# The recurrent stage's small matrix products: grouped by shape, head halves interleaved, fewer decay columns

## The chip, the cores and the metric

The kernel runs on one core of one Trainium2 chip, as one program. The metric is the device time of one execution in microseconds (us). The five engines work side by side: TensorE (PE: matrix products, its weight loads shown as PEld), VectorE (DVE), ScalarE (ACT), GpSimd (POOL) and SyncE (SP, which here issues the weight transfers).

## The reference, cut to what matters

Two transformer-like blocks work one after the other on 256 tokens of width 2048, all in float32. The first block has four kinds of attention and a gated feed-forward layer. The second has three branches; the change touches only the middle one, a recurrent time mix with 16 heads of width 64:

```python
w = -jax.nn.softplus(-(f(w0) + jnp.tanh(wd) @ f(w2))) - 0.5
decay = jnp.exp(-jnp.exp(w))
...
def step(state, inp):                      # one token, per head
    r_t, w_t, k_t, v_t, a_t, b_t = inp
    sa = jnp.einsum('bhij,bhj->bhi', state, a_t)
    state = state * w_t[:, :, None, :] + sa[..., None] * b_t[:, :, None, :] + v_t[..., None] * k_t[:, :, None, :]
    return state, jnp.einsum('bhij,bhj->bhi', state, r_t)
```

The kernel computes this in chunks of 64 tokens: within a chunk the products of all pairs of tokens are made at once (a "Gram" matrix per head and chunk), a triangular system is solved, and the 64x64 state is carried from chunk to chunk.

## The kernel before, in words

**The dense stream.** All wide projections (`unit_b`, `unit_a`) read their weights from HBM in pieces of 128x1024 float32 (512 KB, issued by SP at L291). ACT rounds a piece to a float32r copy `Wh` (L293), DVE makes the remainder `Wl` (L294). For each piece TensorE does 8 products with `Wh` (512 columns: activations in two parts) and 8 with `Wl` (256 columns), into the PSUM tiles `pd`. This stream runs from the first to the last microsecond, and every other piece of work is a small task that advances by one `yield` after each dense piece (`step`). All tiles `ps` are the side tasks' own four PSUM buffers. Every product is issued by the helper `mm` (L189) and every transpose by the helper `tr` (L193), so the trace shows these two lines and the tiles tell the work apart.

**The recurrent stage.** The 16 heads are 8 pairs: pair i has its two heads (h = 0, 1) on partitions 0-63 and 64-127. Four pairs are a group, so there are two groups; 256 tokens are 4 chunks.

- `rw_pre(i)`, for each of 8 pairs: the decays. `sig` (tokens by features) is multiplied by a constant triangle; `tri2` holds two of them side by side, one that includes the token itself and one that excludes it, so one product gives 256 columns. ACT takes the exponentials (L1215, both halves in one instruction, and L1217). Then come the Gram products (L1262): 4 chunks for head 0 on rows 0-63, then 4 for head 1 on rows 64-127; DVE masks each head's PSUM tile (L1265) and POOL writes a part of it to DRAM.
- `rw_solve`, `rw_merge`: the triangular solve, not touched.
- `rw_scan(g, c)`, for each group and chunk, 8 heads each: the values are brought to time-major order (below "V"; L1357 a product with the identity for head 0, L1358 a transpose for head 1, in turn); products `pw`, `pu`, `pn` with `yield`s between them; last the output `po` (L1407 and L1408): for every head the state's share (64 rows) and then the chunk's own share (128 rows), in turn, the second accumulating on the first. In chunk 0 there is no state's share.

In the trace a float32 product is two MATMUL records and a transpose is one; so 8 products of 64x64 are "x16". In the rows, `ps<-e,s` with 128*64 is `pn`, `ps<-s,q` with 64*64 is the state's share of `po`, `ps<-s,e` with 128*64 is the chunk's own share, `ps<-con,s` with 64*64 is V, `ps<-s,b` is the Gram product and `ps<-con,b` the four transposes after it.

**What sets the order.** The tile framework lists instructions per engine from the order of the code, by its own estimate of readiness; an instruction given to `pin` keeps its place. Each engine then works its list strictly in order.

Of the kernel before, what the change touches and what calls it, by code (L numbers as in the profile page):

```python
# [13 lines left out]
AF = mybir.ActivationFunctionType  # L14
OP = mybir.AluOpType
# [10 lines left out]
EM05 = float(np.exp(-0.5))  # L26
# [7 lines left out]
def shape_constants():  # L34

    p = np.arange(128)[:, None]
    c = np.arange(256)[None, :]
    dist = (128 + p - c).astype(np.float32)
    causal = dist >= 0

    def table(slope, ok):
        return np.where(ok, -np.float32(slope) * dist, np.float32(NEG)).astype(np.float32)

    def slopes(n):
        return (2.0 ** (-8.0 * np.arange(1, n + 1) / n)).astype(np.float32)

    tabs = [table(0.0, causal)]
    tabs += [table(s, causal) for s in slopes(8)]
    for h, s in enumerate(slopes(9)):
        win, dil = ((128, 1), (512, 4), (2048, 16))[h // 3]  # L50
        tabs.append(table(s, causal & (dist % dil == 0) & (dist <= win)))
    tabs += [table(s, causal) for s in slopes(4)]
    tabs = np.stack(tabs)

    i = np.arange(128)
    s64, c64 = i % 64, i // 64
    cons = {}
    cons["ident"] = np.eye(128)
    cons["ones"] = np.ones((128, 128))
    cons["bones"] = (c64[:, None] == c64[None, :])  # L60
    cons["anti"] = np.eye(128)[::-1]
    same = c64[:, None] == c64[None, :]
    incl = same & (s64[:, None] <= s64[None, :])
    excl = same & (s64[:, None] < s64[None, :])
    cons["tri2"] = -EM05 * np.concatenate([incl, excl], 1)
    cons["trif"] = (i[:, None] <= i[None, :])
    t64 = np.arange(64)
    cons["gmask"] = np.concatenate([s64[:, None] < t64[None, :], s64[:, None] <= t64[None, :]], 1)
    lm = []
    for b in (16, 32):  # L70
        lm.append((s64[:, None] // (2 * b) == t64[None, :] // (2 * b))
                  & (s64[:, None] // b % 2 == 0) & (t64[None, :] // b % 2 == 1))
    cons["lmask"] = np.concatenate(lm, 1)
    cons["qeye"] = np.tile(np.eye(16).reshape(1, 256), (128, 1))
    sel = np.zeros((128, 7, 128))
    for h in range(7):
        sel[h, h] = 1.0
    cons["sel7"] = sel.reshape(128, 896)
    cons["vmask"] = (i[:, None] // 16 == np.arange(8)[None, :])
    ctab = np.full((128, 2, 8, 16), NEG)  # L80
    cm = np.zeros((128, 2, 16))
    for qt in range(2):
        tq = qt * 128 + np.arange(128)
        dc = (tq[:, None] - (np.arange(15) * 16 + 31)[None, :]).astype(np.float32)
        for h, s in enumerate(slopes(8)):
            ctab[:, qt, h, :15] = np.where(dc >= 0, -s * dc, NEG)
        cm[:, qt, :15] = dc >= 0
    cons["ctab"] = ctab.reshape(128, 256)
    cons["cmask"] = cm.reshape(128, 32)
    out, off = [], {}  # L90
    for phase in PHASES:
        cols, parts = 0, []
        for k in phase:
            v = np.asarray(cons[k], np.float32)
            off[k] = (cols, v.shape[1])
            cols += v.shape[1]
            parts.append(v)
        out.append(np.ascontiguousarray(np.concatenate(parts, 1), np.float32))
    return tabs, out, off
# [2 lines left out]
PHASES = (("ident", "ones", "bones", "anti"),  # L102
          ("trif", "vmask", "ctab", "cmask"),
          ("sel7",),
          ("tri2", "gmask", "lmask"),
          ("qeye",))
TABS, CONST, COFF = shape_constants()

# [39 lines left out]
class Build:  # L148
# [1048 lines left out]
    def rw_pre(self, i, raw):  # L1197

        nc, v = self.nc, self.nc.vector
        V = self.V  # L1200
        st = self.rw[i] = {"vb": self.slot()}
        r, k, vv = (self.rw_lerp(raw[j], i, j) for j in range(3))
        del raw
        yield

        p = self.ps()
        p3 = p.rearrange("p (x t) -> p x t", x=2)
        for tt in range(2):
            self.mm(p3[:, :, tt * 128:tt * 128 + 128],
                    self.sig[tt][i // 4][:, (i % 4) * 128:(i % 4) * 128 + 128],  # L1210
                    self.C["tri2"].rearrange("p (x t) -> p x t", x=2))
        two = self.tmp((128, 1024), tag="b2")
        dec = two[:, :512]
        Pt, Pe = dec[:, :256], dec[:, 256:]
        nc.scalar.activation(dec, p, AF.Exp)  # L1215
        Pi = self.tmp()
        nc.scalar.activation(Pi, p[:, :256], AF.Exp, scale=-1.0)  # L1217
        st["pc"] = self.tiny(4)
        v.tensor_copy(st["pc"], Pt[:, 63:256:64])

        p = self.ps()[:, :256]
        self.mm(p, self.a2[i // 4][64:128, (i % 4) * 128:(i % 4) * 128 + 128], self.lad[64:128, :])
        a = self.tmp()
        nc.scalar.activation(a, p, AF.Tanh, scale=0.5, bias=V["a0"][:, i:i + 1])
        v.tensor_scalar(a, a, 0.5, 0.5, op0=OP.mult, op1=OP.add)

        q = self.tmp()
        nc.scalar.activation(q, k, AF.Square, scale=V["kk"][:, i:i + 1])
        yield
        p = self.ps()[:, :256]  # L1230
        self.mm(p, self.C["bones"], q)
        x = self.tmp()
        v.tensor_scalar(x, p, 1e-24, None, op0=OP.max)
        kn = self.tmp()
        self.rsqrt(kn, x, q)
        v.scalar_tensor_tensor(kn, k, V["kk"][:, i:i + 1], kn, op0=OP.mult, op1=OP.mult)
        ar = st["ar"] = self.slot((128, 4, 2, 64))
        bk = two[:, 512:].rearrange("p (c x t) -> p c x t", c=4, x=2)
        c4 = lambda t: t.rearrange("p (c t) -> p c t", c=4)
        v.scalar_tensor_tensor(ar[:, :, 0, :], c4(kn), -1.0, c4(Pe), op0=OP.mult, op1=OP.mult)  # L1240
        v.tensor_tensor(ar[:, :, 1, :], c4(r), c4(Pt), op=OP.mult)
        v.tensor_tensor(kn, kn, a, op=OP.mult)
        v.tensor_scalar(a, a, V["ka"][:, i:i + 1], self.ka1[:, i:i + 1], op0=OP.mult, op1=OP.add)
        v.tensor_tensor(k, k, a, op=OP.mult)
        for h in range(2):
            s = slice(64 * h, 64 * h + 64)
            v.tensor_tensor(bk[s, :, h, :], c4(kn[s]), c4(Pi[s]), op=OP.mult)
            v.tensor_tensor(bk[s, :, 1 - h, :], c4(k[s]), c4(Pi[s]), op=OP.mult)

        v.scalar_tensor_tensor(q, r, V["rk"][:, i:i + 1], k, op0=OP.mult, op1=OP.mult)  # L1250
        yield
        p = self.ps()[:, :256]
        self.mm(p, self.C["bones"], q)
        st["bv"] = st["vb"][:, 256:]
        v.tensor_tensor(st["bv"], p, vv, op=OP.mult)
        st["v"] = vv

        gm = st["gm"] = [self.slot((128, 4, 128)) for _ in range(2)]
        for h in range(2):
            s = slice(64 * h, 64 * h + 64)  # L1260
            p = self.ps()
            for c in range(4):  # L1262
                self.mm(p[:, c * 128:c * 128 + 128], bk[s, c].rearrange("p x t -> p (x t)"),
                        ar[s, c].rearrange("p x t -> p (x t)"))
            v.tensor_tensor(gm[h], p.rearrange("p (c t) -> p c t", c=4),  # L1265
                            self.C["gmask"][:, None, :].to_broadcast([128, 4, 128]), op=OP.mult)
            nc.gpsimd.dma_start(self.rd[i // 4, h, i % 4].rearrange("c s t -> s c t"), gm[h][s, :, 0:64])
        yield
        p = self.ps()
        for c in range(4):  # L1270
            self.tr(p[:, c * 128:c * 128 + 128], bk[:, c].rearrange("p x t -> p (x t)"))
        st["bkt"] = self.slot((128, 4, 128))
        nc.scalar.copy(st["bkt"], p.rearrange("p (c t) -> p c t", c=4))
# [68 lines left out]
    def rw_scan(self, g, c):  # L1342

        nc, v = self.nc, self.nc.vector
        R = [self.rw[4 * g + j] for j in range(4)]
# [8 lines left out]
        uv = [half(), half()]  # L1354
        p = self.ps().rearrange("p (j h t) -> p j h t", j=4, h=2)
        for j in range(4):
            self.mm(p[64:128, j, 0, :], R[j]["vb"][0:64, cs], self.ident[0:64, 0:64])  # L1357
            self.tr(p[0:64, j, 1, :], R[j]["vb"][64:128, cs], 64)  # L1358
        nc.scalar.copy(uv[0][64:128], p[64:128, :, 0, :])
        nc.scalar.copy(uv[1][0:64], p[0:64, :, 1, :])  # L1360
        yield
# [24 lines left out]
        if c < 3:  # L1386
# [13 lines left out]
            else:  # L1400
                v.tensor_tensor(sn, pn, bc, op=OP.mult)
            self.rwst = sn
        po = quad()
        for j in range(4):
            for h in range(2):
                s = hs[h]
                if c:  # L1407
                    self.mm(po[s, j, :], ST[s, j, :], R[j]["ar"][s, c, 1, :], True, False)  # L1408
                self.mm(po[s, j, :], uv[h][:, j, :], R[j]["gm"][h][:, c, 64:128], not c, True)
        for a in range(2):  # L1410
            nc.scalar.copy(O[a][:, :, cs], po[:, 2 * a:2 * a + 2, :])

# [375 lines left out]
```

## Time and profile before

| | |
|---|---|
| median of 3 runs | 2567.84 us (2560.59 to 2719.17) |
| the profiled execution | 2565.86 us, span 2563.7 us |
| PE busy | 2478.7 us, 97% of the span |
| PEld busy | 2124.7 us, 83% |
| DVE busy | 1793.0 us, 70% |
| ACT busy | 1294.2 us, 50% |
| mean granted TensorE clock | 0.981 of full speed |
| weights read | 516.60 MB, 205 GB/s over the span |

In the profile's 40 slices TensorE is at 9 tenths or more from the eighth on with one exception; the first slices are those in which DMA is at 9 tenths. The recurrent stage lies between about 1430 and 2050 us. A busy TensorE is not the same as a fully used one: a small product shows its whole pass through the array as busy, and beside the dense stream only the distance from one record's start to the next says what it cost.

### The profile page before, as it was taken

The page shows a single profiled execution, that of the slowest core. Times are in us where ns is not written, and L with a number is a line of the kernel's source. Part 1 is how long each engine was busy: PE and PEld are TensorE (multiplying, and loading weights), DVE is VectorE, ACT ScalarE, POOL GpSimd, SP SyncE. Part 2 cuts the span into 40 slices and gives each one's busy share as a digit, 9 for nine tenths or more (in the row PEclk, how much of TensorE's full clock was granted, in tenths as well). Part 3 has the DMA queues.
Part 4 walks back from the last instruction along what each step waited for, and adds up shares of the span by engine and source line. Part 5 has one row for each costly group of instructions (what it writes and reads, how often), then busy time and mean ns, then how long its engine had stood idle before and what let it go on. Part 6 is the DMA issues. An engine that isn't in the chain of part 4 may idle for free.

```text
span 2563.7 us, 39188 instructions
## 1 busy us (share of the span) xinstructions
PE 2478.7 (97%) x14820; PEld 2124.7 (83%) x14820; DVE 1793.0 (70%) x3371; ACT 1294.2 (50%) x2177; POOL 55.7 (2%) x102
## 2 busy tenths in 40 slices
PE   6889999998799999999999999999999999999999
PEld 5678888777688888888888878888888888888888
DVE  8987777689767765555566887659885666666664
ACT  5354455665544444444455554546553554444443
POOL 0000000000000000000000002000110000000000
PEclk8999999999899999999999999999999999999999
DMA  9998777678578866666655656324554366666675
GB/s 326 340 341 286 247 240 267 203 232 270 181 247 277 277 212 190 192 189 188 188 183 183 204 177 181 108 79 149 166 157 124 97 193 189 189 188 190 189 229 166
DMA packets 161500, 527.57 MB, mean 206 GB/s; under 512 B 22912, under 2 KB 33175, under 8 KB 161184
## 3 DMA queue, kind: packets, MB, share of 16 engines
q1 hardware_dynamic: 157296, 516.41, 62.7%
q0 software_dynamic: 4016, 8.66, 1.1%
q8 instruction: 116, 1.90, 0.3%
q14 instruction: 72, 0.59, 0.1%
HBM read 516.60 MB, written 9.45 MB: 205 GB/s over the span
## 4 chain that ended last, share of the span: by engine, by line
PE 71%; issue 12%; DVE 8%; DMA 5%; ACT 2%; POOL 1%; SPq 0%; DVEq 0%; ACTq 0%; POOLq 0%
PE pd L189 64%; PE ps L189 6%; DVE Wl L294 3%; DVE b L432 2%; DMA b<-in_ada_w_dram 2%; DMA W<-in_w_mem_kv_dram 1%; DMA W<-in_w_out_dram 1%; ACT Wh L293 1%; PE ps L193 1%; DMA W<-in_w_in_dram 1%; POOL q L1283 0%; DMA tq<-qd 0%; DVE dt L224 0%; DVE e L590 0%; DVE q L1061 0%
## 5 line engine op out<-in xcount | busy, mean ns | idle before, releaser
L189 PE MATMUL pd<-s,Wh 128*128 128x512 f32 (+1 forms) x5824 | 1450.2, 391 | 37.5 <-ACT Wh L293 19.1
L294 DVE TENSOR_TENSOR Wl<-W,Wh 128x1024 fp32r<-128x1024 f32 x770 | 927.8, 1207 | 546.7 <-ACT Wh L293 519.8
L293 ACT CAST Wh<-W 128x1024 fp32r<-128x1024 f32 x770 | 796.8, 1036 | 957.6 <-PE pd L189 596.7
L189 PEld LDWEIGHTS pd<-s,Wh 128*128 128x128 f32 x5824 | 1032.5, 192 | 225.9 <-ACT Wh L293 24.1
L189 PEld LDWEIGHTS pd<-s,Wl 128*128 128x128 f32 x5584 | 769.4, 192 | 65.8 <-DVE Wl L294 11.2
L189 PE MATMUL pd<-s,Wl 128*128 128x256 f32 x5584 | 795.8, 285 | 6.8 <-DVE Wl L294 6.7
L432 DVE SCALAR_TENSOR_TENSOR b<-b,tq 128x1024 f32<-128x1024 f32 x192 | 233.0, 1221 | 51.0 <-DMA b<-in_ada_w_dram 50.7
L189 PE MATMUL pd<-Wh,s 128*128 128x512 f32 (+4 forms) x576 | 164.0, 363 | 4.3 <-ACT Wh L293 4.3
L189 PEld LDWEIGHTS pd<-Wh,s 128*128 128x128 f32 x576 | 103.8, 189 | 21.7 <-ACT Wh L293 6.2
L224 DVE TENSOR_TENSOR dt<-pd,dt 128x256 f32<-128x256 f32 x289 | 110.7, 418 | 11.0 <-ACT dt L223 10.3
L189 PE MATMUL pd<-Wl,s 128*128 128x512 f32 (+4 forms) x288 | 105.2, 365 | 5.5 <-DVE Wl L294 5.5
L223 ACT COPY dt<-pd 128x256 f32<-128x256 f32 x289 | 94.6, 370 | 22.8 <-PE pd L189 20.9
L189 PE MATMUL ps<-s 128*128 128x256 f32 (+7 forms) x356 | 88.7, 384 | 4.4 <-DVE tab L1555 2.3
L189 PEld LDWEIGHTS ps<-s 64*128 64x128 f32 (+4 forms) x356 | 57.4, 192 | 27.8 <-issue 13.7
L189 PEld LDWEIGHTS pd<-Wl,s 128*128 128x128 f32 x288 | 54.7, 190 | 16.1 <-DVE Wl L294 8.9
L594 ACT ACTIVATE e<-e,y 128x256 f32<-128x256 f32 x80 | 35.7, 449 | 30.3 <-DVE y L592 30.3
L189 PE MATMUL ps<-q,con 128*128 128x256 f32 x132 | 40.0, 410 | 8.4 <-ACT q L1033 2.9
L209 DVE TENSOR_TENSOR s<-q,s 128x256 fp32r<-128x256 f32 x104 | 40.0, 421 | 5.0 <-ACT s L208 4.7
L208 ACT CAST s<-q 128x256 fp32r<-128x256 f32 x104 | 37.9, 405 | 8.2 <-DVE q L1084 4.9
L189 PE MATMUL ps<-pt,s 128*64 128x128 f32 (+3 forms) x176 | 37.6, 343 | 1.7 <-ACT pt L609 1.7
L600 ACT ACTIVATE e<-e,y 128x256 f32<-128x256 f32 x88 | 35.0, 450 | 6.5 <-DVE y L632 3.8
L590 DVE CUSTOM_DVE_ANT_0 e<-ps,tab 128x256 f32<-128x256 f32 x80 | 26.1, 352 | 16.4 <-PE ps L189 16.1
(291 smaller groups left out, 1400.0 us busy)
## 6 DMA issues: line engine op xcount, KB each, us to landing
W<-in_w_in_dram SPq DMA_DIRECT2D x334, 512.0 KB, 3.7
b<-in_ada_w_dram SPq DMA_DIRECT2D x192, 512.0 KB, 5.4
W<-in_ffn_w_gate_dram SPq DMA_DIRECT2D x88, 512.0 KB, 3.8
W<-in_ffn_w_up_dram SPq DMA_DIRECT2D x88, 512.0 KB, 4.1
W<-in_ffn_w_down_dram SPq DMA_DIRECT2D x80, 512.0 KB, 3.6
W<-in_w_mem_kv_dram SPq DMA_DIRECT2D x32, 512.0 KB, 6.4
W<-in_w_out_dram SPq DMA_DIRECT2D x32, 512.0 KB, 4.4
W<-in_w_o_dram SPq DMA_DIRECT2D x32, 512.0 KB, 4.2
```

Of the source, the lines that this page charges most:

```text
L189: self.nc.tensor.matmul(out, lhsT, rhs, start=start, stop=stop)
L193: self.nc.tensor.transpose(out, in_, self.ident[p0:p0 + n, p0:p0 + n])
L208: self.nc.scalar.copy(out[:, :256], src)
L209: self.nc.vector.tensor_tensor(out[:, 256:], src, out[:, :256], op=OP.subtract)
L223: self.nc.scalar.copy(t, ps[:, 256:512])
L224: self.nc.vector.tensor_tensor(t, ps[:, :256], t, op=OP.add)
L293: nc.scalar.copy(Wh[:, :n], W[:, :n])
L294: nc.vector.tensor_tensor(Wl[:, :n], W[:, :n], Wh[:, :n], op=OP.subtract)
L432: nc.vector.scalar_tensor_tensor(W, W, 1.0, self.crow[half], op0=OP.mult, op1=OP.mult, accum_out=acc[:, k:k + 1])
L590: nc.vector.tensor_tensor_reduce(e[:, lo:hi], p[:, lo:hi], tab[:, t0:256], scale=1.0, scalar=-3e38, op0=OP.add, op1=OP.max, accum_out=m[:, ...
L594: nc.scalar.activation(e[:, lo:hi], e[:, lo:hi], AF.Exp, bias=nm[:, a:a + 1], accum_out=sm[:, a:a + 1])
L600: self.nc.scalar.activation(e[:, lo:hi], e[:, lo:hi], AF.Copy, scale=f[:, a:a + 1])
```

## The change

Four things, all in the recurrent stage.

1. Decay: the constant `tri2` (256 columns) becomes `tri` (128 columns, the inclusive triangle). The exclusive decays are the inclusive ones moved by one token: ACT writes the exponentials to columns 1 to 64 of a 65-column tile per chunk, DVE sets column 0 to 1 (a new pinned memset), and the two are read at offsets 0 and 1.
2. Gram: the two heads' products alternate, into two PSUM tiles taken at once; the two maskings follow after all eight.
3. V: head 1 is brought to time-major order by a product with the identity instead of a transpose.
4. Output of the scan: first all eight products with the state, then all eight of the chunk's own share, all accumulating in the one PSUM tile; only the first pair starts it afresh.

```diff
-    excl = same & (s64[:, None] < s64[None, :])
-    cons["tri2"] = -EM05 * np.concatenate([incl, excl], 1)
+    cons["tri"] = -EM05 * incl
...
-        p = self.ps()
-        p3 = p.rearrange("p (x t) -> p x t", x=2)
+        c4 = lambda t: t.rearrange("p (c t) -> p c t", c=4)
+        p = self.ps()[:, :256]
         for tt in range(2):
-            self.mm(p3[:, :, tt * 128:tt * 128 + 128],
-                    self.sig[tt][i // 4][:, (i % 4) * 128:(i % 4) * 128 + 128],
-                    self.C["tri2"].rearrange("p (x t) -> p x t", x=2))
+            self.mm(p[:, tt * 128:tt * 128 + 128],
+                    self.sig[tt][i // 4][:, (i % 4) * 128:(i % 4) * 128 + 128], self.C["tri"])
         two = self.tmp((128, 1024), tag="b2")
-        dec = two[:, :512]
-        Pt, Pe = dec[:, :256], dec[:, 256:]
-        nc.scalar.activation(dec, p, AF.Exp)
+
+        dec = two[:, :260].rearrange("p (c t) -> p c t", c=4)
+        self.pin(v.memset(dec[:, :, 0:1], 1.0))
+        Pt, Pe = dec[:, :, 1:65], dec[:, :, 0:64]
+        nc.scalar.activation(Pt, c4(p), AF.Exp)
         Pi = self.tmp()
-        nc.scalar.activation(Pi, p[:, :256], AF.Exp, scale=-1.0)
+        nc.scalar.activation(Pi, p, AF.Exp, scale=-1.0)
         st["pc"] = self.tiny(4)
-        v.tensor_copy(st["pc"], Pt[:, 63:256:64])
+        v.tensor_copy(st["pc"], dec[:, :, 64])
...
         gm = st["gm"] = [self.slot((128, 4, 128)) for _ in range(2)]
+        pg = [self.ps(), self.ps()]
+        for c in range(4):
+            for h in range(2):
+                s = slice(64 * h, 64 * h + 64)
+                self.mm(pg[h][:, c * 128:c * 128 + 128], bk[s, c].rearrange("p x t -> p (x t)"),
+                        ar[s, c].rearrange("p x t -> p (x t)"))
         for h in range(2):
             s = slice(64 * h, 64 * h + 64)
-            p = self.ps()
-            for c in range(4):
-                self.mm(p[:, c * 128:c * 128 + 128], bk[s, c].rearrange("p x t -> p (x t)"),
-                        ar[s, c].rearrange("p x t -> p (x t)"))
-            v.tensor_tensor(gm[h], p.rearrange("p (c t) -> p c t", c=4),
+            v.tensor_tensor(gm[h], pg[h].rearrange("p (c t) -> p c t", c=4),
                             self.C["gmask"][:, None, :].to_broadcast([128, 4, 128]), op=OP.mult)
...
         for j in range(4):
-            self.mm(p[64:128, j, 0, :], R[j]["vb"][0:64, cs], self.ident[0:64, 0:64])
-            self.tr(p[0:64, j, 1, :], R[j]["vb"][64:128, cs], 64)
+            for h in range(2):
+                s, o = hs[h], hs[1 - h]
+                self.mm(p[o, j, h, :], R[j]["vb"][s, cs], self.ident[s, s])
...
         po = quad()
+        if c:
+            for j in range(4):
+                for h in range(2):
+                    s = hs[h]
+                    self.mm(po[s, j, :], ST[s, j, :], R[j]["ar"][s, c, 1, :], j == 0, False)
         for j in range(4):
             for h in range(2):
                 s = hs[h]
-                if c:
-                    self.mm(po[s, j, :], ST[s, j, :], R[j]["ar"][s, c, 1, :], True, False)
-                self.mm(po[s, j, :], uv[h][:, j, :], R[j]["gm"][h][:, c, 64:128], not c, True)
+                self.mm(po[s, j, :], uv[h][:, j, :], R[j]["gm"][h][:, c, 64:128], not c, j == 3 or not c)
```

The order of TensorE's list at the end of chunk 1 of the first group, before. Each row is one instruction of the program, or a run of equal ones, with the shape of its moving operand; `ps<-e,s` is `pn`, then follow `po` and V of the next chunk.

```order
L189 MATMUL ps<-e,s 64x64 x8
L189 MATMUL ps<-s,q 64x64
L189 MATMUL ps<-s,e 64x64
...
L189 MATMUL ps<-con,s 64x64
L193 MATMUL ps<-con,s 64x64
...
L189 MATMUL pd<-s,Wh 128x512 x8
L189 MATMUL pd<-s,Wl 128x256 x8
```

The same place in the changed kernel (its helper lines stand one line higher: L188, L192):

```order
L188 MATMUL ps<-e,s 64x64 x8
L188 MATMUL ps<-s,q 64x64 x8
L188 MATMUL ps<-s,e 64x64 x8
L188 MATMUL ps<-con,s 64x64 x8
L188 MATMUL pd<-s,Wh 128x512 x8
```

Sixteen products that alternated between two shapes now stand as two runs of eight, and the four products and four transposes of V as one run of eight products; the dense pieces around them keep their places, give or take a few products. In chunk 3 of the second group the list still puts a few dense products between the parts of the second run.

TensorE's list around the Gram products of the first pair, before (`b_14097` is the tile that holds decays and Gram operands):

```order
L189 MATMUL ps<-s,b_14097 128x128 x8
L193 MATMUL ps<-con,b_14097 128x128 x4
L189 MATMUL ps<-s 128x2x128 x2
L189 MATMUL ps<-s 128x256
L189 MATMUL pd<-s,Wh 128x512 x5
```

and in the changed kernel:

```order
L188 MATMUL ps<-s,b_14097 128x128 x8
L192 MATMUL ps<-con,b_14097 128x128 x4
L188 MATMUL ps<-s 128x128 x2
L188 MATMUL pd<-s,Wh 128x512
L188 MATMUL ps<-s 128x256
```

The decay products of the next pair (`128x2x128`, two runs of 128 columns) became `128x128`, and one dense product now stands between them and the next product of the same pair.

## Rows read from the trace of the kernel before

**Rows 1.** The page, part 1: busy time, share of the span, records.

```profile
PE 2478.7 (97%) x14820; PEld 2124.7 (83%) x14820; DVE 1793.0 (70%) x3371; ACT 1294.2 (50%) x2177; POOL 55.7 (2%) x102
```

**Rows 2.** Windows: stretch, its length, busy per engine, granted clock, DMA share, GB/s.

```profile
1660.00:1670.00 10.00, 10.00 (x114) 8.39 (x112) 5.53 (x14) 6.22 (x14) 0.00 (x0) 1.00 0.52 165
1670.00:1725.00 55.00, 55.00 (x426) 44.23 (x425) 25.49 (x67) 25.68 (x55) 0.00 (x0) 0.91 0.26 82
1682.00:1684.00 2.00, 2.00 (x6) 1.54 (x6) 0.00 (x0) 0.00 (x0) 0.00 (x0) 0.50 0.00 0
1980.00:2035.00 55.00, 55.00 (x412) 43.98 (x411) 27.94 (x61) 23.84 (x51) 0.00 (x0) 0.91 0.26 80
2050.00:2100.00 50.00, 50.00 (x288) 43.98 (x287) 34.67 (x55) 25.75 (x42) 0.00 (x0) 1.00 0.67 198
```

**Rows 3.** Longest waits of PE (1430 to 1650) and PEld (1900 to 2050): total, times, longest.

```profile
PE ps L189 <- DVE tab L1555: 2.3, 1, 2.3
PEld ps L189 <- issue: 0.7, 2, 0.4
```

**Rows 4.** Lines by form, 1430 to 2050: record counts | busy us, mean ns.

```profile
L189 PE MATMUL ps<-s,q 64*64 64x64 f32 x96 | 15.7, 244 | 0.0
L189 PE MATMUL ps<-s,b 64*128 64x128 f32 x128 | 13.7, 285 | 0.0
L189 PE MATMUL ps<-con,s 64*64 64x64 f32 x64 | 10.8, 251 | 0.0
L193 PE MATMUL ps<-con,s 64*64 64x64 f32 x32 | 8.0, 250 | 0.0
```

**Rows 5.** Timeline of PE, end of chunk 1, group 0: start us, length us, record.

```profile
1674.42 0.69 PE L189 MATMUL ps<-e,s 128*64 128x64 f32 x16
1675.04 0.33 PE L189 MATMUL ps<-s,q 64*64 64x64 f32 x2
...
1679.14 0.32 PE L189 MATMUL ps<-con,s 64*64 64x64 f32 x2
1679.40 0.24 PE L193 MATMUL ps<-con,s 64*64 64x64 f32 x1
...
1680.85 3.59 PE L189 MATMUL pd<-s,Wh 128*128 128x512 f32 x8
1684.23 1.25 PE L189 MATMUL pd<-s,Wl 128*128 128x256 f32 x8
```

**Rows 6.** Timeline of PE, earlier in the same group: runs of one shape, and chunk 0.

```profile
1650.79 0.68 PE L189 MATMUL ps<-e,s 64*64 64x64 f32 x16
1651.40 2.11 PE L189 MATMUL pd<-s,Wh 128*128 128x512 f32 x8
...
1655.03 0.68 PE L189 MATMUL ps<-q,tq 64*64 64x64 f32 x16
1655.65 2.14 PE L189 MATMUL pd<-s,Wh 128*128 128x512 f32 x8
1657.62 1.10 PE L189 MATMUL pd<-s,Wl 128*128 128x256 f32 x8
...
1660.82 0.69 PE L189 MATMUL ps<-e,s 128*64 128x64 f32 x16
...
1663.62 0.92 PE L189 MATMUL ps<-pt,s 128*128 128x256 f32 x4
```

**Rows 7.** Timeline of PE and PEld at the Gram products of pair 0.

```profile
1477.20 1.71 PE L189 MATMUL ps<-s,b 64*128 64x128 f32 x16
1478.84 0.66 PE L193 MATMUL ps<-con,b 128*128 128x128 f32 x4
1479.34 1.66 PE L189 MATMUL ps<-s 128*128 128x256 f32 x6
1480.29 0.29 PEld L189 LDWEIGHTS ps<-s 64*128 64x128 f32 x2 [0.33 <-issue]
```

**Rows 8.** Lines by form on DVE, 1430 to 2050.

```profile
L1448 DVE MEMSET e<- 128x1 f32 x22 | 1.3, 59 | 0.0
```

More of the change, by code (lines that the diff above doesn't have):

```diff
@@ L104 @@
           ("sel7",),
-          ("tri2", "gmask", "lmask"),
+          ("tri", "gmask", "lmask"),
           ("qeye",))
@@ L1238, in rw_pre @@
         bk = two[:, 512:].rearrange("p (c x t) -> p c x t", c=4, x=2)
-        c4 = lambda t: t.rearrange("p (c t) -> p c t", c=4)
-        v.scalar_tensor_tensor(ar[:, :, 0, :], c4(kn), -1.0, c4(Pe), op0=OP.mult, op1=OP.mult)
-        v.tensor_tensor(ar[:, :, 1, :], c4(r), c4(Pt), op=OP.mult)
+        v.scalar_tensor_tensor(ar[:, :, 0, :], c4(kn), -1.0, Pe, op0=OP.mult, op1=OP.mult)
+        v.tensor_tensor(ar[:, :, 1, :], c4(r), Pt, op=OP.mult)
         v.tensor_tensor(kn, kn, a, op=OP.mult)
```

## The prediction

> **What bounds the kernel.** I read the page's first part, then the stretches of the recurrent stage, then the waits, then the timeline of TensorE. TensorE is busy for 97% of the span [rows 1]. In the two scans, which fill 1670 to 1725 and 1980 to 2035 us, and in the dense stretch behind them it is busy without a gap [rows 2], while DVE and ACT are below half in the scans and DMA is at 0.26. The longest waits there are tenths of a microsecond [rows 3]; earlier, among the preparations of the pairs, one of 2.3 us stands out [rows 3]. So in this stage the end moves with TensorE's own list: what a small product takes from one start to the next is paid in full, and what is saved there lets the next dense piece start earlier. The reader should see one more thing: in both scan stretches the granted clock is 0.91, in the stretches around them 1.00 [rows 2].
>
> **What a small product costs now.** At the end of chunk 1, `pn` (eight products of one shape, its two halves alternating) takes from 1674.42 to 1675.04, that is 0.62 us for 16 records. Then the two shapes of `po` alternate: the sixteen products last from 1675.04 to 1679.14, 4.10 us, so 0.26 us from one to the next [rows 5]. V takes from 1679.14 to 1680.85, 1.71 us, with 0.26 us from product to transpose [rows 5]. Runs of one shape elsewhere cost little: eight 64x64 products whose halves alternate take 0.61 us (1650.79 to 1651.40) and 0.62 us (1655.03 to 1655.65) [rows 6]. So it is the change of shape that costs about 0.26 us; as two runs the same sixteen would take less than a third of that.
>
> **The change, part by part.**
>
> *Output of the scan.* Per chunk 4.10 us become one run of 64x64 (0.62, as 1655.03) and one of 128x64 (0.62, as `pn`): 1.24, a saving of 2.86 us. There are 96 records with the state, so 48 products, so six chunks of eight [rows 4]: 6 x 2.86 = 17.2 us. Both prices are those of the same shapes in the same stage; I take no range for them. In the second group's chunk 3 the second run stays cut once by dense products, which costs one change of shape, 0.26 us, and stays inside the rounding. The accumulation flags change no instruction.
>
> *V.* 64 + 32 records are 32 products and 32 transposes [rows 4], eight chunks of four each. They become eight products of 64x64 that cross from one half of the partitions to the other; the products at 1650.79 do that too (`pw`: rows of one half, result in the other) and cost 0.61 [rows 6]. Four more records per chunk are in that price. 8 x (1.71 - 0.61) = 8.8 us.
>
> *Gram.* 128 records are 64 products, eight pairs of eight [rows 4]; one pair takes 1477.20 to 1478.84, 1.64 us [rows 7], head 0 first. No row shows alternating halves with 128 columns. Bounds: no gain at all (0; a loss is rival 3's case), or twice as fast (0.82 us a pair). The nearest rows are the alternating 64x64 runs, 0.62 us for as many records [rows 6]; twice the columns of weights and of moving data would make at most 1.24. Entry into the run and exit from it don't double, so I take 1.14, a saving of 0.5: 8 x 0.5 = 4.0 us, between 0 and 6.6.
>
> *Decay.* The two products (four records) take 1479.34 to 1480.29, where the next weight load starts: 0.95 us; the other two of the six records are the next product. Four records of 128x128 take 1478.84 to 1479.34, 0.50 us [rows 7]. 8 x 0.45 = 3.6 us. ACT's exponential shrinks from 512 to 256 columns, which frees time on an engine that doesn't bound. The new memset on DVE, four columns, is near 59 ns [rows 8], eight times, 0.5 us in all under the dense products. It is queued ahead of `Wl` pieces, so if its tile were not free it would hold those back; its predecessors there are transfers and transposes of three tiles earlier, and I cost it at nothing. Uncovered it would be 0.5 us.
>
> *The two PSUM tiles of Gram.* The first tile is now masked after all eight products and not after four, but the eight end sooner. What is queued behind is the next pair's decay, which needs the buffers in the same turn as before; the list now has one dense product in between. I cost it at nothing; a wait would be at most the mask of one head.
>
> *The clock.* The dense eight behind V take 3.38 us (1680.85 to 1684.23) where they take 1.97 at full clock (1655.65 to 1657.62) [rows 5, 6], and the granted clock is 0.50, the 1.2 GHz level, in 1682 to 1684 [rows 2]. This comes after 6.4 us of small products (1674.42 to 1680.85) [rows 5]. In the two scans the clock averages 0.91 over 55 us each, so 2 x 55 x 0.09 = 9.9 us of clock are lost [rows 2]. After chunk 0 it does not fall: there `pn`, half a `po` and V, 1660.82 to 1663.62, 2.80 us, are followed by work at 1.00 [rows 6, 2]. With the change such a stretch of chunk 1 lasts 0.62 + 1.24 + 0.61 = 2.47 us, shorter than the one after which the clock held. I expect the falls to go, and take 9 of the 9.9 us, since some of the halved time was fill that doesn't scale; the bounds are 0 and 9.9.
>
> *A rule against it.* In the new runs both halves write into one PSUM tile, and the products at 1655.03 do the same: there 16 records take 0.62 us [rows 6]. The Trainium skill, TensorEngine Tiling (Array Packing), Restrictions and Gotchas, Gotcha 1, says that different row tiles cannot access the same PSUM bank simultaneously. By it the products with the state and V would run one half after the other, which is the second rival below; the trace does not bear it out.
>
> **The sum.** 17.2 + 8.8 + 4.0 + 3.6 + 9 = 42.6 us. The profiled execution took 2565.86 us, of which 2563.7 are the span; 2565.86 - 42.6 = 2523.3. The median of the runs shown is 2567.84, 2 us above the profiled one, so against it this is 1.7% less. Behind the scans TensorE is busy 50.00 of 50 us [rows 2], so nothing later gives it back: the weights come at 198 GB/s there, and in the scans, where the pace rises, they came at 80.
>
> **Rivals.**
>
> 1. *The clock falls all the same.* For: between the small runs there are dense ones of only 2 to 3 us, and what makes the clock fall is not told by a row. Against: chunk 0. Then 2523 + 9 = 2532.
> 2. *The halves don't run side by side in one bank* (the rule above). Then a 64-row run goes at the pace of head 0's Gram products, 1.64 us for 16 records [rows 7]. V saves 8 x 0.07 = 0.6, `po` 6 x (4.10 - 1.64 - 0.62) = 11.0, Gram nothing, decay 3.6, and the clock still falls after stretches of 4.5 us: 15 us, 2551. Against: the two runs of rows 6.
> 3. *Slower: alternating halves cost as much as a change of shape.* If every alternation in the new runs cost p per product, the saving is 6 x (4.10 - 16p) + 8 x (1.71 - 8p) + 8 x (1.64 - 8p) + 3.6 = 55 - 224p: it turns into a loss above p = 0.246 us, and at the 0.257 (4.10 / 16) of `po` it is 2.6 us slower, 2568, with the clock as before. Against: the same rows, 0.62 / 8 = 0.08 per product.
> 4. *The preparations wait for DVE instead.* There TensorE did wait for DVE once for 2.3 us [rows 3]; what Gram and decay save (7.6 us) could turn into more such waits, for the masks and for operands that DVE makes pair by pair. Then 2531.
> 5. *More than the sum.* Gram twice as fast (+2.6), all of the clock (+0.9), and runs 5 us below the profiled one, as the lowest of before (2560.59) is: 2523 - 8.5 = 2514.5, which is over 2% below the median.
>
> **Chances and range.** Forecast 0.60, rival 1 0.11, rival 2 0.04, rival 3 0.02, rival 4 0.08, rival 5 0.15. The forecast's own case is about 2517 to 2530 (Gram's bounds and the spread of runs). The range takes in rivals 1 and 4 with some room, and nearly reaches rival 5's low end: 2512 to 2539. About 2% is what a measurement of this kernel can tell from no change, 51 us, and my sum lies just inside it. Faster by over 2%: rival 5 and a little of the forecast, 0.20; within 2%: 0.78; slower by over 2%: 0.02, since rival 3 at its own price stays within 2%.
>
> **What would show it.** `po` of a chunk as two runs of about 0.62 us each in the timeline; V as 16 records in 0.6; Gram in 1.1 us per pair and decay's four records in 0.5; the clock at 1.00 through both scans; TensorE still without gaps there. The forecast is wrong if the runs of eight take over 1 us, if the clock shows 0.91 again, if DVE's memset or masks appear as waits of TensorE, or if the dense stretch behind the scans starts to wait for weights.

## The result and the profile after

The changed kernel took 2527.14 us in the median of 4 runs (2525.21 to 2534.44), the kernel before 2564.49 beside it. One of the four runs of before took 2719.17 us, 6% more than the fastest, and is left out of the ratio, which is 0.9865, 95% interval 0.9832 to 0.9897: faster by about 35 us, or 1.35%, clear of no change but less than 2%. Forecast were 2523.3, so 42.6 us less than the profiled execution of before.

The profiled execution of the change took 2534.44 us (span 2532.7), the longest of its four. To see what the change did, I cut both traces at the same dense products, which both kernels run in the same order, and took the time from one to the next:

| stretch | before | after | difference |
|---|---|---|---|
| first dense product to the recurrent stage | 1412.58 | 1419.45 | +6.87 |
| preparations of the pairs, groups 0 and 1 | 355.24 | 351.39 | -3.85 |
| merges of the chunks | 123.29 | 120.02 | -3.27 |
| scan, group 0 | 61.90 | 46.34 | -15.56 |
| scan, group 1 | 74.47 | 58.43 | -16.04 |
| last 500 us | 500.01 | 500.01 | 0.00 |

The recurrent stage, which is the four middle rows, became 38.7 us shorter. Ahead of it both kernels issue the same instructions; what that stretch lost is the spread from run to run (below, in the last section). The table leaves out the 12.6 and 13.4 us ahead of the first dense product. Behind the scan of group 1 both traces take 518.8 us to TensorE's last record, of which it shows 500.

The page of after, part 1, answers to [rows 1]:

```profile
PE 2440.0 (96%) x14852; PEld 2094.4 (83%) x14852; DVE 1792.8 (71%) x3379; ACT 1292.7 (51%) x2177; POOL 55.6 (2%) x102
```

TensorE is busy 38.7 us less. Now the end of chunk 1 of group 0 in TensorE's timeline after (start us, length us, record), which answers to [rows 5]:

```profile
1678.20 0.69 PE L188 MATMUL ps<-e,s 128*64 128x64 f32 x16
1678.81 0.68 PE L188 MATMUL ps<-s,q 64*64 64x64 f32 x16
1679.42 0.69 PE L188 MATMUL ps<-s,e 128*64 128x64 f32 x16
1680.04 0.68 PE L188 MATMUL ps<-con,s 64*64 64x64 f32 x16
1680.65 2.11 PE L188 MATMUL pd<-s,Wh 128*128 128x512 f32 x8
1682.60 0.99 PE L188 MATMUL pd<-s,Wl 128*128 128x256 f32 x7
```

From start to start, `po` is two runs of 0.61 and 0.62 us, 1.23 where it was 4.10, and V is 0.61 where it was 1.71. The dense eight behind them take 1.95 us where they took 3.38. The windows over both scans and the dense stretch behind (columns as in [rows 2]) show the rest:

```profile
1671.00:1717.00 46.00, 46.00 (x469) 39.31 (x468) 31.53 (x84) 29.11 (x60) 0.00 (x0) 1.00 0.37 110
1951.00:2010.00 59.00, 58.97 (x601) 50.30 (x600) 42.24 (x90) 34.33 (x70) 0.00 (x0) 1.00 0.36 110
2019.00:2069.00 50.00, 50.00 (x288) 43.96 (x288) 34.21 (x55) 26.06 (x43) 0.00 (x0) 1.00 0.64 197
```

The clock is at 1.00 in both scans instead of 0.91, TensorE still has no gaps there, and the weights behind them come in time. This is the forecast's picture. The picture among the preparations is different. The windows from the first preparation of a group to the end of its merges, before:

```profile
1425.20:1671.12 245.92, 240.85 (x1613) 201.73 (x1612) 187.23 (x401) 128.56 (x199) 23.43 (x41) 0.99 0.53 163
1733.02:1965.63 232.61, 230.20 (x1556) 196.97 (x1554) 190.14 (x425) 130.36 (x219) 19.68 (x34) 1.00 0.50 150
```

and after:

```profile
1432.88:1674.90 242.02, 235.53 (x1622) 197.50 (x1620) 186.72 (x405) 128.19 (x199) 23.42 (x41) 0.99 0.53 165
1721.23:1950.62 229.39, 225.51 (x1559) 193.13 (x1558) 190.16 (x429) 129.66 (x219) 19.64 (x34) 1.00 0.49 152
```

Subtract the busy time of PE (the second number) from the length (the first): TensorE's idle time was 5.07 + 2.41 = 7.5 us and is 6.49 + 3.88 = 10.4. Its work there shrank by 10.0 us, the stretch by 7.1. DVE is busy for 77% and 83% of these stretches. What TensorE waits for in the first of them (engine, tile, line <- releaser: total us, times, longest) is DVE above all:

```profile
PE ps L188 <- DVE s L1553: 2.1, 1, 2.1
PE ps L188 <- DVE q L1249: 1.1, 2, 0.7
PE ps L188 <- DVE s L1266: 0.9, 2, 0.8
```

L1553 scales normalised queries and keys of the attention heads and is no part of the change. L1249 makes the operand of the bonus product, which stands right ahead of Gram in TensorE's list. L1266 masks Gram's result; before the change PE shows no wait for the masks in either stretch, and after it 0.9 us in the first and 0.2 in the second. The wait for the operand of the bonus product was there before:

```profile
PE ps L189 <- DVE q L1250: 0.9, 2, 0.5
```

With the second stretch it was 1.6 us in all and is 2.7.

Yet Gram itself is as short as forecast. The first pair of group 1 in TensorE's timeline after:

```profile
1768.30 0.67 PE L188 MATMUL ps<-q,con 128*128 128x256 f32 x2 [0.45 <-DVE e L1455]
1768.90 1.16 PE L188 MATMUL ps<-s,b 64*128 64x128 f32 x16
1769.99 0.66 PE L192 MATMUL ps<-con,b 128*128 128x128 f32 x4
1770.49 0.61 PE L188 MATMUL ps<-s 128*128 128x128 f32 x4
1770.85 0.47 PE L188 MATMUL pd<-s,Wh 128*128 128x512 f32 x1
```

The 16 records last 1.09 us, where [rows 7] had 1.64 (1.14 was forecast), and decay's four take 0.36 up to the next dense product, where they took 0.95 up to the next weight load; the two ends differ, so this overstates the saving.

### The profile page after: what moved, and what is told of

It is laid out like the page before. It is cut to its first block, busy times and chain, and to the rows that moved or that the text cites. A ratio compares the mean times of both kernels' runs of the same rounds, so it can differ in the third digit from the quotient of the medians.

```text
span 2532.7 us, 39262 instructions
## 1 busy us (share of the span) xinstructions
PE 2440.0 (96%) x14852; PEld 2094.4 (83%) x14852; DVE 1792.8 (71%) x3379; ACT 1292.7 (51%) x2177; POOL 55.6 (2%) x102
## 4 chain that ended last, share of the span: by engine, by line
PE 75%; DVE 11%; DMA 8%; issue 3%; ACT 2%; SPq 0%; ACTq 0%; DVEq 0%
PE pd L188 67%; PE ps L188 8%; DVE Wl L293 4%; DMA b<-in_ada_w_dram 4%; DVE b L431 2%; DMA W<-in_w_in_dram 2%; DMA W<-in_w_mem_kv_dram 1%; ACT Wh L292 1%; DMA W<-in_w_out_dram 1%; PE ps L192 1%; DVE dt L223 0%; DVE q L202 0%; DVE q L201 0%; DVE s L208 0%; DVE b L1247 0%
## 5 line engine op out<-in xcount | busy, mean ns | idle before, releaser
L188 PE MATMUL pd<-s,Wh 128*128 128x512 f32 (+1 forms) x5824 | 1447.8, 390 | 40.0 <-ACT Wh L292 20.2
L188 PEld LDWEIGHTS pd<-s,Wh 128*128 128x128 f32 x5824 | 1030.2, 191 | 228.0 <-ACT Wh L292 25.7
L188 PEld LDWEIGHTS pd<-s,Wl 128*128 128x128 f32 x5584 | 765.5, 191 | 66.7 <-DVE Wl L293 12.8
L188 PE MATMUL pd<-s,Wl 128*128 128x256 f32 x5584 | 791.9, 284 | 8.0 <-DVE Wl L293 7.8
L188 PE MATMUL pd<-Wh,s 128*128 128x512 f32 (+4 forms) x576 | 164.4, 363 | 3.6 <-ACT Wh L292 3.5
L188 PEld LDWEIGHTS pd<-Wh,s 128*128 128x128 f32 x576 | 103.9, 190 | 20.9 <-ACT Wh L292 5.9
L223 DVE TENSOR_TENSOR dt<-pd,dt 128x256 f32<-128x256 f32 x289 | 110.6, 418 | 12.1 <-ACT dt L222 11.8
L188 PE MATMUL pd<-Wl,s 128*128 128x512 f32 (+4 forms) x288 | 105.5, 366 | 6.8 <-DVE Wl L293 6.8
L188 PE MATMUL ps<-s 64*128 64x256 f32 (+7 forms) x356 | 84.8, 369 | 5.2 <-DVE s L1553 3.0
L188 PEld LDWEIGHTS ps<-s 64*128 64x128 f32 (+4 forms) x356 | 55.0, 187 | 28.1 <-issue 11.6
L188 PEld LDWEIGHTS pd<-Wl,s 128*128 128x128 f32 x288 | 54.6, 189 | 18.2 <-DVE Wl L293 11.1
L188 PE MATMUL ps<-q,con 128*128 128x256 f32 x132 | 39.4, 404 | 10.7 <-ACT q L1032 3.0
L188 PEld LDWEIGHTS ps<-q,con 128*128 128x128 f32 x132 | 22.7, 193 | 19.8 <-ACT q L519 4.5
L188 PE MATMUL ps<-pt,s 128*64 128x128 f32 (+3 forms) x176 | 37.4, 341 | 1.7 <-ACT pt L608 1.7
L599 ACT ACTIVATE e<-e,y 128x256 f32<-128x256 f32 x88 | 34.9, 449 | 7.5 <-DVE y L798 3.8
```

The source lines that it names most:

```text
L188: self.nc.tensor.matmul(out, lhsT, rhs, start=start, stop=stop)
L223: self.nc.vector.tensor_tensor(t, ps[:, :256], t, op=OP.add)
L599: self.nc.scalar.activation(e[:, lo:hi], e[:, lo:hi], AF.Copy, scale=f[:, a:a + 1])
```

## The experiments

Two theories stood. **Price of runs:** a change of shape on TensorE costs about 0.26 us, the clock falls follow long stretches of such changes, and both are paid in full in the scans; this gives 35 us. **Preparations:** what Gram and decay save on TensorE turns mostly into waiting for DVE. The rivals stand in the expectations. Where one trace is compared with another, the time is the recurrent stage cut as above (after: 576.2 us), since the stretch ahead of it varies. In the runs of the changed kernel and of experiments 1, 3 and 4, the instructions of preparations and merges are the same, and the two together took 471.4, 470.6, 472.1 and 472.8 us: 2.2 us of spread, which is what single traces can resolve there. The scans repeat to 0.1 us where nothing in them was changed.

**1. The output's products alternate again** (all else as in the change).

```
-        if c:
-            ...                 # the eight products with the state, as a run of their own
         for j in range(4):
             for h in range(2):
+                if c:
+                    self.mm(po[s, j, :], ST[s, j, :], R[j]["ar"][s, c, 1, :], True, False)
-                self.mm(po[s, j, :], uv[h]..., not c, j == 3 or not c)
+                self.mm(po[s, j, :], uv[h]..., not c, True)
```

> The changed kernel with the scan's output products in the old order again (state's share and chunk's share in turn for each head). All figures are the time between the same two dense products around the recurrent stage, against the changed kernel. Theory (each change of shape costs about 0.26 us): 6 chunks x (4.10 - 1.24) = 17 us longer, and the stretch of small products is 0.62 + 4.10 + 0.61 = 5.3 us, long enough for the clock to fall again, so 17 plus up to 9, about 24. Rival (the clock falls only with the transposes of V in the stretch): 17 and the granted clock stays at 1.00 through both scans.

One run took 2546.47 us. The stage is 597.0 us, 20.9 longer than after, of which the scan of group 0 has 13.3 and that of group 1 8.3. TensorE's timeline at the end of chunk 1:

```profile
1669.20 0.33 PE L188 MATMUL ps<-s,q 64*64 64x64 f32 x2
1669.45 0.33 PE L188 MATMUL ps<-s,e 128*64 128x64 f32 x2
...
1673.30 0.68 PE L188 MATMUL ps<-con,s 64*64 64x64 f32 x16
```

and the windows over the two scans and over one of the falls of the clock:

```profile
1663.00:1724.00 61.00, 61.00 (x479) 50.28 (x479) 33.74 (x90) 30.02 (x61) 0.00 (x0) 0.92 0.29 89
1942.00:2010.00 68.00, 68.00 (x663) 56.25 (x663) 36.78 (x70) 31.27 (x65) 0.00 (x0) 1.00 0.35 106
1708.50:1715.20 6.70, 6.70 (x22) 5.11 (x21) 1.64 (x5) 2.38 (x5) 0.00 (x0) 0.50 0.18 70
```

The sixteen products take 4.10 us again. Group 1 shows their price alone, since its clock stays at 1.00: 8.3 us for three chunks, 2.8 each, as the term of 2.86 has it. Group 0 has 5 us more, and the clock at 0.92: it is at half from 1691.4 us on, 5.1 us after the small products of chunk 2 began, and from 1708.4 on, 3.0 us after the alternating products of chunk 3 began. It did not fall after the 5.3 us of chunk 1 in group 0, nor in group 1, where chunks 1 and 2 have 5.3 us as well. So the length of the stretch alone does not tell where the clock falls.

**2. V by products and transposes again.**

```
         for j in range(4):
-            for h in range(2):
-                s, o = hs[h], hs[1 - h]
-                self.mm(p[o, j, h, :], R[j]["vb"][s, cs], self.ident[s, s])
+            self.mm(p[64:128, j, 0, :], R[j]["vb"][0:64, cs], self.ident[0:64, 0:64])
+            self.tr(p[0:64, j, 1, :], R[j]["vb"][64:128, cs], 64)
```

> The changed kernel with V as product and transpose in turn again. Theory: V back at 1.71 us, 8 x 1.1 = 8.8 us longer; the stretch is 0.62 + 1.24 + 1.71 = 3.6 us, little above the 2.8 us after which the clock held, so the clock stays at 1.00: 8.8 in all. Rival (it was the transposes that let the clock fall): the clock falls in both scans, up to 9 us more, 18 in all.

One run took 2526.87 us; the stage is 584.6, 8.4 longer than after. Scans and merges, where the eight V's are, are 8.8 longer (the preparations 0.4 shorter, within their spread); the term was 8.8. The end of chunk 1 in TensorE's timeline:

```profile
1666.35 0.32 PE L188 MATMUL ps<-con,s 64*64 64x64 f32 x2
1666.61 0.24 PE L192 MATMUL ps<-con,s 64*64 64x64 f32 x1
...
1668.06 0.73 PE L188 MATMUL pd<-s,Wh 128*128 128x512 f32 x2
```

V lasts 1.71 us. The clock stays at 1.00 in both scans, after stretches of 3.6 us. That the whole run is no longer than after comes from its first 700 us, which took 679.0 us instead of 691.2 with the same instructions.

**3. Alternating, with the accumulation drawn apart.** The two products that add into one place stand seven or nine products apart, and shapes still alternate. The rival was that adding to a result just written is what takes time, and not the change of shape.

```
+            jh = [(j, h) for j in range(4) for h in range(2)]
+            for n, (j, h) in enumerate(jh):
+                ...  # product with the state for (j, h)
+                j, h = jh[(n + 4) % 8]
+                ...  # the chunk's own share for that (j, h)
```

> The changed kernel with the scan's output products alternating between the two shapes as before the change, but each chunk-share product now adds to a place that was written eight products away, not to the place written just before (the order of the chunk-share products is turned by four). Theory (the price is that of the change of shape): 4.1 us per chunk as before the change, 17 us longer plus the clock's falls, like the plain alternation. Rival (the second product waited for the first to leave the array, since it adds to the same place): about 1.2 us per chunk and no difference to the changed kernel.

One run took 2549.73 us; the stage is 599.9, 23.7 longer than after. TensorE's timeline at the end of chunk 1:

```profile
1670.34 0.32 PE L188 MATMUL ps<-s,q 64*64 64x64 f32 x2
1670.60 0.33 PE L188 MATMUL ps<-s,e 128*64 128x64 f32 x2
...
1674.45 0.68 PE L188 MATMUL ps<-con,s 64*64 64x64 f32 x16
```

Again 4.11 us, so the rival falls. Here the clock fell in both groups (0.97 and 0.93 over the scans), 13.6 us at half clock in all.

**4. Runs of two.** Per pair of heads, both products with the state, then both shares of the chunk.

```
-            for j in range(4):
+        for j in range(4):
+            if c:
                 for h in range(2):
                     self.mm(po[s, j, :], ST[s, j, :], ..., j == 0, False)
-        for j in range(4):
             for h in range(2):
                 self.mm(po[s, j, :], uv[h][:, j, :], ...)
```

> The changed kernel with the scan's output products in eight runs of two per chunk (both heads of a pair with the state, then both heads' chunk share), so half as many changes of shape as before the change. Theory (one price per run, both halves of a run side by side): 8 x 0.26 = 2.06 us per chunk against 1.24, 6 x 0.82 = 4.9 us longer; stretch 0.62 + 2.06 + 0.61 = 3.3 us, clock at 1.00. Rival (the price is per product, not per run): 4.1 us per chunk, 17 us longer.

One run took 2534.89 us. The timeline of the same place:

```profile
1673.20 0.33 PE L188 MATMUL ps<-s,q 64*64 64x64 f32 x4
1673.47 0.34 PE L188 MATMUL ps<-s,e 128*64 128x64 f32 x4
...
1675.31 0.68 PE L188 MATMUL ps<-con,s 64*64 64x64 f32 x16
```

Eight runs of two take 2.11 us, 0.26 each, as much as a run of one. So the price goes by the run and hardly by the products in it, as long as these are one on each half. The two scans are 5.4 us longer than after; six chunks by 2.11 - 1.23 make 5.3. No fall of the clock.

**5. and 6. Gram head by head again; decay with the double triangle again.** Each alone.

```
-        for c in range(4):          # Gram, experiment 5
-            for h in range(2):
+        for h in range(2):
+            for c in range(4):
...
-    self.mm(p[:, tt * 128:tt * 128 + 128], ..., self.C["tri"])    # decay, experiment 6
+    self.mm(p3[:, :, tt * 128:tt * 128 + 128], ..., self.C["tri2"]...)
```

> The changed kernel with the Gram products of head 0 first and then those of head 1 (still into two tiles taken at once). The alternating run took 1.09 us per pair where it had been 1.64. Theory (about half of what Gram and decay save turned into waits for VectorE in the preparations): 2 us longer over the stage. Rival (Gram's saving is paid in full and something else, the memset or the split of the decay's neighbour, costs the rest): 8 x 0.55 = 4.4 us longer.

> The changed kernel with the decay from the two triangles again (256 columns, no memset). Theory (half of the saving turned into waits for VectorE): 1 to 2 us longer. Rival (the decay's saving came through in full): 3.6 us longer. Second rival (the memset in VectorE's queue and the split list cost more than the decay saved): shorter than the changed kernel.

One run each: 2528.82 and 2523.91 us. Preparations and merges took 470.2 and 470.6 us, where the change took 471.4. Undoing one of the two costs nothing that can be seen, whichever it is: TensorE is busy longer (464.2 and 463.7 us for 461.0) and idle for 6.0 and 6.8 us instead of 10.4, so the longer products fill time in which it waits otherwise.

**7. Both undone at once**, so that only output and V are changed (Gram's two tiles are still taken at once and masked after all eight products).

> The change without Gram and without decay: only V and the scan's output are as changed. With either one of the two left in, the preparations and merges together took 470.2 and 470.6 us, with both 471.4, before the change 478.5 (3.3 of that is V). Theory (the first 4 to 5 us that TensorE saves there come through, what goes beyond waits for VectorE): without both the saving of the preparations is gone, about 475 us, stage 4 to 5 us longer than with either alone. Rival (what came through there has nothing to do with Gram and decay but with the list's order after V and the output changed): about 470 to 471 us as with either.

One run took 2526.31 us. The windows over preparations and merges of this kernel:

```profile
1421.96:1664.38 242.42, 238.81 (x1621) 200.46 (x1620) 186.88 (x401) 128.98 (x199) 23.46 (x41) 0.99 0.55 165
1710.72:1942.06 231.34, 229.08 (x1559) 196.31 (x1557) 190.06 (x425) 130.52 (x219) 19.61 (x34) 1.00 0.50 151
```

They last 473.8 us, 2.4 more than after (1 more than the longest of the four like it), with TensorE busy 467.9 and idle 5.9. So Gram and decay take 6.8 us off TensorE's work (7.6 were forecast), add 4.5 us of idle time, and bring 2.4, give or take a microsecond. The traces of before and after gave 3.85 for the same two (the preparations in the table): experiment 7 took 353.8 us for the preparations where before, with the same products there, took 355.2. So 2.4 to 3.9 us arrived.

**8. Less work for DVE.** The key's inverse root straight from ACT, without the refinement that DVE does on it; this leaves out the refinement's three DVE operations, eight times.

```
-        self.rsqrt(kn, x, q)
+        nc.scalar.activation(kn, x, AF.Abs_reciprocal_sqrt)
```

> The changed kernel without the three VectorE instructions that refine the inverse norm of the keys in the preparations (it leaves that refinement out): 8 x 3 x 0.42 = 10 us less VectorE work there and 1.2 us less on each pair's chain to the Gram operands; TensorE's work is the same. Theory (in the preparations TensorE waits for VectorE, 2.9 us more than before the change): 2 to 4 us shorter over the stage. Rival (the rest of the missing saving is in changes of shape of the list itself): no difference within 1 us.

One run took 2524.44 us. The windows:

```profile
1425.08:1664.84 239.76, 234.83 (x1621) 197.90 (x1620) 183.05 (x393) 128.08 (x199) 23.40 (x41) 0.99 0.55 167
1711.18:1940.69 229.51, 225.49 (x1559) 193.51 (x1558) 185.81 (x417) 130.33 (x219) 19.57 (x34) 1.00 0.50 152
```

DVE works 8.0 us less (368.9 for 376.9), the stretches are 2.1 us shorter, and TensorE's idle time goes from 10.4 to 9.0. That is the low end of what the theory gave and about as large as the spread, so by itself it shows little: 8 us less of DVE's work brought 2 at most.

**9. A wait taken away by order.** The Gram products ahead of the bonus product, which waits for `q` of L1249.

```
         yield
-        p = ...; self.mm(p, self.C["bones"], q); ...   # bonus
         gm = ...                                       # Gram's eight products
+        p = ...; self.mm(p, self.C["bones"], q); ...
```

> The changed kernel with the Gram products ahead of the bonus product, whose operand VectorE makes last. Theory (TensorE waited for that operand, 2.7 us in all in the trace of the changed kernel): about 3 us shorter over the stage. Rival (the wait moves to the next operand that VectorE makes, the Gram operands or the masks): no difference within 1 us.

Median 2524.85 us of 4 (2522.78 to 2526.52; ratio to before 0.9841, 0.9821 to 0.986). The longest waits of TensorE in the first preparations, in this kernel:

```profile
PE ps L188 <- DVE tab L1562: 1.8, 1, 1.8
PE ps L188 <- ACT q L1540: 0.8, 1, 0.8
PE ps L188 <- DVE b L1247: 0.6, 2, 0.4
```

The wait for `q` of L1249 is gone. Preparations and merges take 468.5 us, 3.0 less than after and 2.2 less than the shortest of the four like it; TensorE idles there for 5.3 us instead of 10.4, but is busy for 2.1 more. This shows better than experiment 8 that waiting for a particular result of DVE costs time in the preparations. That it was this wait which took the change's saving it shows only in part: of the 2.7 us that TensorE waited for this operand, 1.6 were there before the change.

**10. More runs of one shape: the merges.** The products `pz` and `pq` of the merges went head by head; now the heads alternate.

```
-            for h in range(2):
-                for c in range(4):
+            for c in range(4):
+                for h in range(2):
                     self.mm(pz[s, c * 64:c * 64 + 64], ro[m][s, c, :], t[s, c, 0, :])
...              # pq likewise, each of its two kinds over both heads
```

> A version beyond the change: in the triangular merge, too, the two heads' 64x64 products alternate instead of head 0 first. Theory (halves side by side take one step of 0.058 us for two records): per two pairs 32 records 1.46 to 1.12 us three times and 64 records 3.34 to about 2.05 us: 4 x 2.3 = 9 us shorter over the stage, about 0.36% of the time. Rival (the steps of the merge are ordered by ScalarE and VectorE between them, and the saving turns into waits): 0 to 3 us shorter.

Median 2516.71 us of 4 (2512.90 to 2517.75; ratio to before 0.9805, 0.9788 to 0.9822). The stage is 567.0 us, 9.2 shorter than after.

**11. Both of them,** 9 and 10.

> The changed kernel with both further edits: the merge's halves alternating (9.2 us shorter over the stage when alone) and Gram ahead of the bonus product (3.0 us when alone). Theory (they save at different places of TensorE's list): 12 us shorter over the stage, about 2514 us. Rival (both draw on the same slack of VectorE in the preparations): 9 to 10 us, no faster than the merge edit alone.

Median 2513.96 us of 4 (2511.82 to 2515.86; ratio 0.9797, 0.9781 to 0.9814): this version beats both kernels, 13 us below the change and 51 below the kernel before; whether it is faster than before by over 2% the interval leaves open. Its stage is 564.4 us, 11.8 shorter than after, near 9.2 + 3.0. Its windows over preparations and merges:

```profile
1422.39:1657.07 234.68, 230.00 (x1621) 193.52 (x1620) 186.49 (x405) 127.72 (x199) 23.50 (x41) 1.00 0.55 171
1703.42:1928.30 224.88, 222.31 (x1559) 190.02 (x1557) 189.04 (x429) 129.99 (x219) 19.59 (x34) 1.00 0.51 155
```

DVE is now busy for 79% and 84% of them.

**12. The same, with one more operation moved from DVE to ACT.**

```
-        v.tensor_scalar(a, a, 0.5, 0.5, op0=OP.mult, op1=OP.add)
+        nc.scalar.activation(a, a, AF.Copy, scale=0.5, bias=0.5)
```

> The version with both further edits, and the scaling of one gate (128x256, 0.29 us, 8 times) moved from VectorE to ScalarE. Theory (VectorE is what the preparations wait for): 0.5 to 2 us shorter over the stage than without that move. Rival (0.29 us a pair is below what the list's order makes of it): no difference, or a little longer since ScalarE's copy takes about 0.4 us in the same chain.

Median 2515.63 us of 4 (2509.54 to 2517.25; ratio 0.98, 0.9777 to 0.9823), the stage 564.3 us: no difference to 11. This operation was on no path that TensorE waits for.

## Why the prediction was right, and the step that failed

*Output of the scan (17.2).* Right. Per chunk 4.10 became 1.23, and experiment 1 gives it back without the clock: 8.3 us in group 1, so 16.7 for both.

*V (8.8).* Right: experiment 2 gives back 8.8 in scans and merges.

*The clock (9).* Right, near its upper bound. Scans and merges lost 34.9 us together (15.6 + 16.0 + 3.3); less 16.7 and 8.8 this leaves 9.4. The stretch of small products is 2.5 us now, and the clock held. That the falls would go was right; that it is the length of the stretch which makes them is not shown. With `po` in runs of eight or of two the clock also held after stretches of 3.6 us (2) and 3.3 us (4), and in the merges of the changed kernel it held through 4.8 us of 64x64 products (1912.26 to 1917.02). Where the shapes of `po` alternated (1 and 3), it fell 3.0 to 5.1 us into the stretch in some places, once right behind a stretch of 3.3 us, and held through 5.3 us in others. These three terms are 35.0 in the sum and 34.9 in the traces.

*The rule against it.* The second rival is out: into one PSUM tile, products of both halves take 0.61 us for 16 records. Its price of 1.64 us came from Gram, whose products have twice the columns: 64x64 products take 1.47 us for 32 records head by head in the merges of the changed kernel, and 1.08 alternating in experiment 10, so head by head would have cost less than the rival says. The Trainium skill also says (TensorEngine Tiling (Array Packing), Tiling Modes, Key Properties) that a change of the tiling mode, other than one of the tile, drains TensorE. The runs agree and add the price: about 0.26 us a run of `po`, whether it holds one product or two. They do not show that it is the draining which takes this time. A product and a transpose of V, both 64x64, cost 0.43 us a pair, where the same two as products in a run take 0.15.

*Gram and decay (4.0 + 3.6).* The step that failed is the one ahead of the sum, "So in this stage the end moves with TensorE's own list". It was read from windows and waits over the scans and carried over to the preparations, where the one row shown was a wait of 2.3 us for DVE. The product times were right (7.6 forecast, 6.8 taken off TensorE), but only 2.4 to 3.9 us arrived at the end, and either half alone brought as much (experiments 5 to 7). The fourth rival had named this mechanism, with all 7.6 us eaten; half to two thirds were. One of the signs that the prediction had set for itself appeared: waits of TensorE for the masks, 1.1 us in all, where the two PSUM tiles were put at nothing. The memset, put at nothing too, shows up in no wait of TensorE. A window over 1425 to 1671 in the trace of before would have shown TensorE idle for 5 us beside a DVE at 76%, and the order of the list that the bonus product, which waits for DVE, stands ahead of Gram.

*The sum.* In the two traces the stage is 38.7 us shorter where 42.6 were forecast, and the missing 3.9 are Gram and decay. Whole runs differ by about 35 us, but those of one kernel spread over 7 to 9 us, so they can't tell 35 from 39. How close 2527.14 came to 2523.3 therefore says little; the stage does. One reading was off, and nothing rests on it: in the second scan DVE is busy for 27.94 of 55 us, which is just over half and not below.

*What stays open.* How the added idle time splits among DVE's results is not settled. From experiment 7 to the change it grows by 4.5 us; TensorE's waits for the operand of the bonus product grow by 1.1 and those for the masks by 1.1, and the rest lies in several waits below a microsecond each that no run takes apart. Experiment 8 took 8 us of work from DVE and gained about 2, experiment 12 nothing. Why the clock fell in group 0 of experiment 1 and not in group 1, with nearly equal stretches, is not known.

## What to carry to other kernels

Count the runs of one shape in TensorE's list, not the small products: group them by shape, and let the two halves alternate within a run. Look up the granted clock in and behind stretches in which shapes alternate. And before a saving on the busiest engine is put into the sum, read idle time and the next engine's share in that very stretch: where the next one is near 80% and makes operands for the shortened step, move first what waits for it.

## What the runs showed of the hardware that was not expected

- In `po`, a run of one product and a run of two, one for each head, take the same 0.26 us; a run of eight takes 0.61 to 0.62.
- Products with 128 columns also go side by side on the two halves: 1.64 us for 16 records head by head, 1.09 alternating.
- The clock fell to half in or right behind stretches of alternating shapes, in experiment 1 once only 3.0 us after the alternation began, though TensorE shows no gap there: busy is not the same as clocked up.
- The same instructions take different times ahead of the recurrent stage: the first 700 us ranged from 679.0 to 691.2 us over the traces of change and experiments, the last 500 were equal to 0.01. Single runs that differ by 10 us say little about a stage; cut at common products they do.
